# A hybrid decoder layer on one core: another order at its start, a shorter chain for 1/sqrt, and the last column sums on TensorE

## The chip, the core and the metric

The kernel runs on one core of a Trainium2 chip, in one launch. Its engines are TensorE (PE, matrix products), VectorE (DVE), ScalarE (ACT), GpSimd (POOL) and SyncE (SP), which here only issues DMA transfers. Each engine works through its own queue in order; they wait for one another by semaphores. The metric is device time in microseconds (us). Before the change it is 1806.27, the median of three runs.

## The reference

One layer over 1056 positions (1024 of a prompt, 32 of samples), 1024 channels wide, float32 throughout:

```
x = x + 1/2 * SwiGLU_1(RMSNorm(x))          # D_FF = 2816
h = RMSNorm(x);  [q | k | v | u | g] = h @ w_in
    gate = gelu(u) * (tril(W_s) RMSNorm(gelu(g)) + b)      # chunks of 128
    attn = sliding-window attention, 8 heads, ALiBi, sinks
x = x + concat(RMSNorm(attn), RMSNorm(gate)) @ w_out
x = x + 1/2 * SwiGLU_2(RMSNorm(x))
y = RMSNorm(x)                              # the final norm
```

RMSNorm divides each position by the root of the mean square of its channels and multiplies by a gain. SwiGLU is `(silu(h @ wg) * (h @ wu)) @ wd`. The new keys, values and gate rows are outputs too.

## The kernel before

Channels lie on the 128 partitions, in 8 tiles (k); positions lie along the free dimension, in two halves (h = 0, 1) of H = 528, each of two pieces of PC = 264. The three stages are FFN1 (`ffn`, L329, called at L1002), the mixer (projection, attention, gate, output projection) and FFN2 (L1098).

**Products.** A float32 product is done as three products of shorter numbers: each operand is split into a high part (a cast or a scaled copy on ScalarE) and a low part (a subtraction on VectorE). For weights that is `wsplit` (L121 and L122, tiles `raw` to `wb`) and `wload` (`whi`, `wlo`); for the normalised activations it is `P1.split` (L193 writes `xh`, L194 writes `xl`, from x and the gains). A block scheme with seven products in the place of eight (`Blocks`, products `a`, `s1` to `s4`, `12`, `22`) covers the large products. Each product instruction of 128x264 reads one such weight and one such activation.

**1/sqrt.** For a norm, ScalarE squares x (`squares`, L172), the first tile straight into the accumulator, the others into `sq`, which VectorE or GpSimd adds (L176). `rstd` (L143) then lets TensorE sum over the partitions (`pn`, L150), VectorE scales (`gv`, L154 and L155) and calls `tiny_rsqrt` (L133), and TensorE spreads the result over all partitions by products with the identity (`pr`, L165). `tiny_rsqrt` is a guess by integer operations (L136, L137) and three Newton steps of three operations each (L139 to L141), on tiles `gt` and `gr` of 128x5 or smaller. It is called 21 times: 13 from `rstd`, 8 in the gate (tile `gss`, squares `junk` at L814, result used for `gn` at L819).

**The start** (L640 to L662) loads the gains and the first tiles of x and issues ten products of `ones` with itself (`warm`, L645; the profile counts each as two records). It casts the first two weight blocks, splits x for k = 0 to 3, and goes on with the next loads, blocks and splits.

**The end.** FFN2's last group of products runs once for each piece of positions (`pd`, L620); each of its four d steps adds into x on VectorE (L572). `last` and `one` (L1063 to L1096) then square and sum the finished rows and, at d = 3, start `rstd` for the final norm. `put` copies `pr` to `fr` (L1084), VectorE (L1091) and GpSimd (L1089) multiply, and SP stores `y` (L1093). Of three such pieces the last one (piece 2, 264 positions) has no other work beside it.

**What sets the order.** The program text gives priorities only. A scheduler with a cost model places each engine's instructions, inside the mixer together with a table of due times (`I`). So an edit in one place can move instructions of an engine elsewhere.

Of the kernel before, what the change touches and what calls it, by code (L numbers as in the profile page):

```python
# [14 lines left out]
I32 = mybir.dt.int32  # L15
AF = mybir.ActivationFunctionType
ALU = mybir.AluOpType
# [3 lines left out]
D = 1024  # L21
# [19 lines left out]
def build(nc, tc, ctx, A):  # L41
# [16 lines left out]
    V, S, G, PE = nc.vector, nc.scalar, nc.gpsimd, nc.tensor  # L58
# [9 lines left out]
    def tmp(nm, dt=F32):  # L68
        return tp.tile([128, H], dt, tag="tmp", name=nm)

    def pst(nm):
        return ps.tile([128, 512], F32, tag="ps", name=nm)
# [9 lines left out]
    def small(nm, n=4, p=128):  # L82
        return sp.tile([p, n], F32, tag=f"s_{nm}", name=nm, bufs=1 if nm[0] == "s" else 2 if nm[0] == "g" else 3)
# [11 lines left out]
    ones = cp.tile([128, 128], F32, name="ones")  # L95
# [37 lines left out]
    def tiny_rsqrt(a, n):  # L133

        b, c = small("gr", 5)[:, :n], small("gt", 5)[:, :n]
        V.tensor_scalar(c.bitcast(I32), a.bitcast(I32), 1, None, op0=ALU.arith_shift_right)  # L136
        V.tensor_scalar(b.bitcast(I32), c.bitcast(I32), -1, 0x5F3759DF, op0=ALU.mult, op1=ALU.add)  # L137
        for i in range(3):
            V.tensor_mul(c, b, b)  # L139
            V.scalar_tensor_tensor(c, c, -0.5, a, op0=ALU.mult, op1=ALU.mult)  # L140
            V.scalar_tensor_tensor(a if i == 2 else b, c, 1.5, b, op0=ALU.add, op1=ALU.mult)  # L141

    def rstd(acc, o, n, mul, eps, put):  # L143

        full, rest = n // 128, n % 128
        nj = full + (rest > 0)
        p = pst("pn")
        for j in range(nj):
            m = min(128, n - j * 128)
            PE.matmul(p[:m, j:j + 1], lhsT=acc[:, o + j * 128:o + j * 128 + m], rhs=ones[:, 0:1], start=True, stop=True)  # L150
        v = small("gv", 5)
        if rest:
            V.memset(v, 1.0)
            V.tensor_scalar(v[:rest, full:nj], p[:rest, full:nj], mul, eps, op0=ALU.mult, op1=ALU.add)  # L154
        V.tensor_scalar(v[:, :full], p[:, :full], mul, eps, op0=ALU.mult, op1=ALU.add)  # L155
        tiny_rsqrt(v[:, :nj], nj)
        yield 0.3, LAT["rstd"]

        p = pst("pr")
        for j in range(nj):  # L160
            m = min(128, n - j * 128)
            if j == 4:
                put(p, o)
                p = pst("pr2")
            PE.matmul(p[:, j % 4 * 128:j % 4 * 128 + m], lhsT=v[:m, j:j + 1].to_broadcast([m, 128]), rhs=ident[:m, :m], start=True, stop=True)  # L165
        put(p[:, :n] if nj <= 4 else p[:, :rest], o if nj <= 4 else o + 512)
        yield 1.0, 1

    def squares(acc, x, o, n, first, add=None, on=None):
        s = acc[:, o:o + n] if first else tmp("sq")[:, :n]  # L170
        if on is None:
            S.activation(s, x, AF.Square)  # L172
        else:
            on.tensor_mul(s, x, x)
        if not first:
            (add or G).tensor_add(acc[:, o:o + n], acc[:, o:o + n], s)  # L176
# [456 lines left out]
    X = [Quad(f"x{h}", 8) for h in range(2)]  # L633
    P1 = Prep(X, 0, {(1, 3): [0], (2, 2): [1], (2, 3): [0], (2, 7): [1]})
# [5 lines left out]
    load(gains, A["gains"])  # L640
    load_x(0, 0)
    gb_ = Blocks(A["f1_gu"][0, 0], (1, 2))
    pw = pst("warm")
    for _ in range(10):
        PE.matmul(pw[:, :128], lhsT=ones, rhs=ones, start=True, stop=True)  # L645
    load_x(0, 1, 2, 3)
    gb_.load(0, 3)
    gb_.plain("11", "21")
    for k in range(4):
        P1.split(0, k)  # L650
    load_x(0, 4, 5, 6, 7)
    first = [gb_.plain("12", "22")]
# [380 lines left out]
    for job, ahead in zip(jobs, jobs[1:] + [None]):  # L1033
        if job != jobs[0]:
            wnext = weight(*ahead) if ahead else None
        t, h, kind, i = job
# [20 lines left out]
    first = plain_weights(A["f2_gu"])  # L1057
# [3 lines left out]
    fin, ends, pieces = {}, [], [(0, 0, 2), (1, 0, 1), (1, 1, 1)]  # L1061
# [11 lines left out]
    def one(piece, h, o, n, d):  # L1073
        first = piece not in fin
        if first:
            fin[piece] = tmp("facc")
        squares(fin[piece], X[h](d, o, n), 0, n, first, V if piece else G)
        if d != 3:
            return

        def put(p, o2):
            m = p.shape[-1]
            r = tmp("fr")
            S.copy(r[:, :m], p)  # L1084
            for k in range(8):
                x, g = X[h](k, o + o2, m), gains[:, 32 + k:33 + k]
                if k in ON_POOL[piece]:
                    S.activation(x, x, AF.Copy, scale=g)
                    G.tensor_mul(x, x, r[:, :m])  # L1089
                else:  # L1090
                    V.scalar_tensor_tensor(x, x, g, p if piece == 2 else r[:, :m], op0=ALU.mult, op1=ALU.mult)  # L1091
                if k % 2:
                    load(pair(A["y"], k // 2, T0[h] + o + o2, m), X[h].t[k // 2][:, :, o + o2:o + o2 + m])  # L1093
        if piece == 2:
            ends.pop()
        ends.append(rstd(fin[piece], 0, n, 1.0 / D, 1e-6, put))  # L1096

    ffn(X, P2, A["f2_gu"], A["f2_d"], lambda i, h: pair(spill, i, T0[h], H), first, last, tail)  # L1098
    for _ in ends[0]:
# [100 lines left out]
```

## Time and profile before

| | |
|---|---|
| median of 3 runs | 1806.27 us (1805.62, 1806.27, 1806.62) |
| profiled execution | 1804.15 us, of which its span 1802.4 |
| mean granted TensorE clock | 0.99 |
| TensorE busy | 98% of the span |
| VectorE, ScalarE, GpSimd busy | 68%, 41%, 8% |
| HBM traffic | 147 GB/s over the span |

A row of the timeline gives start, busy time, engine, line, operation, `out<-in`, shapes, count, and in brackets the engine's idle time before it with the instruction that ended it. A row of windows gives a stretch, its length, each engine's busy time with its instructions in the order TensorE, its weight loads, VectorE, ScalarE, GpSimd, and then the granted clock, the DMA share and GB/s.

### The profile page before, as it was taken

The numbers are of one execution on the slowest core, as the hardware profiler recorded it, in microseconds if no ns is written. First come the engines' busy times: TensorE is split into PE (matmuls) and PEld (weight loads), VectorE is DVE, ScalarE is ACT, GpSimd is POOL, SyncE is SP. The second block draws the span as 40 slices with busy tenths as digits, with TensorE's granted clock in tenths as the row PEclk, the third lists the DMA queues.
The fourth block names the chain that finished last, engine by engine and source line by source line (L and its number), as shares of the span: only waits on it lengthen the run. The fifth ranks groups of instructions, "written<-read, shape, count | busy, mean of one in ns | idle before, by whom it ended". The sixth has DMA issues, their size and how long they took to land. (4 is left out here: it accounts for less than half of the span.)

```text
span 1802.4 us, 34123 instructions
## 1 busy us (share of the span) xinstructions
PE 1765.7 (98%) x14045; PEld 1729.8 (96%) x14045; DVE 1217.4 (68%) x2171; ACT 740.3 (41%) x1312; POOL 168.6 (9%) x152
## 2 busy tenths in 40 slices
PE   9999999999999999999989999999999999999997
PEld 9999999999999999998878899999999999999997
DVE  7986766676557565486677885986666676457566
ACT  6543333333343453354554644633333333343441
POOL 0000000000000012212212562000000000000110
PEclk9999999999999999999989999999999999999998
DMA  6154544454595344322120222154544454595532
GB/s 237 33 193 160 205 148 149 156 201 140 186 345 179 131 155 144 96 71 64 55 65 28 93 83 95 41 193 157 201 148 154 154 201 137 187 343 188 181 108 97
DMA packets 104460, 266.05 MB, mean 148 GB/s; under 512 B 12384, under 2 KB 15136, under 8 KB 104288
## 3 DMA queue, kind: packets, MB, share of 16 engines
q1 hardware_dynamic: 104304, 263.87, 42.6%
q8 instruction: 110, 1.80, 0.4%
q14 instruction: 46, 0.38, 0.1%
HBM read 190.25 MB, written 74.60 MB: 147 GB/s over the span
## 5 line engine op out<-in xcount | busy, mean ns | idle before, releaser
L430 PE MATMUL pa<-th,wb 128*128 128x264 f32 x2624 | 493.7, 284 | 1.2 <-DVE wb L122 0.6
L430 PEld LDWEIGHTS pa<-th,wb 128*128 128x128 f32 x2624 | 412.3, 188 | 2.6 <-DVE wb L122 0.9
L430 PE MATMUL pa<-tl,wb 128*128 128x264 f32 x1312 | 373.6, 285 | 2.5 <-DVE tl L299 2.5
L620 PE MATMUL pd<-hh,whi 128*128 128x264 f32 x1208 | 343.6, 285 | 0.0
L620 PE MATMUL pd<-hh,wlo 128*128 128x264 f32 x1208 | 343.6, 284 | 0.0
L620 PE MATMUL pd<-hl,whi 128*128 128x264 f32 x1208 | 343.2, 284 | 0.0
L121 ACT CAST wb<-raw 128x512 fp32r<-128x512 f32 x296 | 181.3, 620 | 284.3 <-PE pc L430 82.1
L122 DVE TENSOR_TENSOR wb<-raw,wb 128x512 fp32r<-128x512 f32 x296 | 201.6, 690 | 105.4 <-ACT wb L121 104.8
L430 PEld LDWEIGHTS pa<-tl,wb 128*128 128x128 f32 x1312 | 246.6, 188 | 2.8 <-DVE tl L299 2.7
L430 PE MATMUL pc<-th,wb 128*128 128x264 f32 x1280 | 247.0, 285 | 1.4 <-DVE x L468 0.8
L620 PEld LDWEIGHTS pd<-hh,wlo 128*128 128x128 f32 x1208 | 227.4, 188 | 0.0
L620 PEld LDWEIGHTS pd<-hh,whi 128*128 128x128 f32 x1208 | 227.2, 188 | 0.1
L620 PEld LDWEIGHTS pd<-hl,whi 128*128 128x128 f32 x1208 | 227.2, 188 | 0.0
L430 PEld LDWEIGHTS pc<-th,wb 128*128 128x128 f32 x1280 | 203.3, 188 | 2.0 <-DVE x L468 1.0
L367 DVE TENSOR_TENSOR wlo<-raw,whi 128x1024 fp32r<-128x1024 f32 x82 | 94.7, 1155 | 135.3 <-ACT whi L366 122.5
L430 PE MATMUL pc<-tl,wb 128*128 128x264 f32 x640 | 181.9, 284 | 0.0
L269 DVE TENSOR_TENSOR raw<-raw 128x512 f32<-128x512 f32 x248 | 168.9, 688 | 17.3 <-DMA raw<-f_d 12.3
L366 ACT CAST whi<-raw 128x1024 fp32r<-128x1024 f32 x82 | 79.9, 980 | 217.1 <-PE pd L620 147.0
L130 PE MATMUL pp<-xh,whi 128*128 128x264 f32 x448 | 132.9, 297 | 0.4 <-DVE mx L866 0.4
L130 PE MATMUL pp<-xh,wlo 128*128 128x264 f32 x448 | 128.5, 287 | 0.0
L130 PE MATMUL pp<-xl,whi 128*128 128x264 f32 x448 | 128.2, 286 | 0.0
L430 PEld LDWEIGHTS pc<-tl,wb 128*128 128x128 f32 x640 | 120.3, 188 | 0.3 <-DVE tl L299 0.3
(233 smaller groups left out, 3080.6 us busy)
## 6 DMA issues: line engine op xcount, KB each, us to landing
raw<-f_gu SPq DMA_DIRECT2D x86, 512.0 KB, 4.2
raw<-f_d SPq DMA_DIRECT2D x74, 512.0 KB, 4.0
ws_s<-raw SPq DMA_DIRECT2D x88, 256.0 KB, 2.0
ht<-ht_s SPq DMA_DIRECT2D x40, 528.0 KB, 7.8
raw<-ws_s SPq DMA_DIRECT2D x40, 512.0 KB, 9.0
raw<-w_in SPq DMA_DIRECT2D x28, 512.0 KB, 3.6
ht_s<-m SPq DMA_DIRECT2D x44, 264.0 KB, 2.3
ht<-ht SPq DMA_DIRECT2D x20, 528.0 KB, 3.7
```

The costliest lines, as they stand in the source:

```text
L121: S.copy(w[:, 0], src)
L122: V.tensor_sub(w[:, 1], src, w[:, 0].bitcast(F32))
L130: PE.matmul(p[:, :n], lhsT=w[a][:, c:c + 128], rhs=b(k, o, n), start=(3 * i + j == 0), stop=(3 * i + j == last))
L269: V.tensor_add(b[dst], b[dst], b[x])
L366: S.copy(wh[:, :n * 512], raw[:, :n * 512])
L367: V.tensor_sub(wl[:, :n * 512], raw[:, :n * 512], wh[:, :n * 512].bitcast(F32))
L430: PE.matmul(ps_[:, j], lhsT=w[:, a, kk * 128:(kk + 1) * 128], rhs=b[kk // 2][c][:, kk % 2, j * PC:(j + 1) * PC], start=(start and kk == 0 ...
L620: PE.matmul(ps_[d][:, j], lhsT=w[:, k * 512 + d * 128:k * 512 + (d + 1) * 128], rhs=t[:, k, j * PC:(j + 1) * PC], start=(bi == 0 and oi == ...
```

## The change

1. **Start.** Twelve warm products in the place of ten, by a helper `busy`. The split of x's tile k = 0 is written ahead of the other loads of x and of the weights' casts.
2. **1/sqrt.** Another integer constant and two steps with other constants: nine VectorE operations in the place of eleven, in all 21 calls.
3. **Last piece.** The squares of its last step (d = 3) go to a tile of their own and aren't added by VectorE. TensorE sums the accumulator and then that tile into the same `pn`.
4. **Last piece.** `busy(4)` follows the first group of these sums in the text, `busy(7)` the second.

```diff
-        V.tensor_scalar(b.bitcast(I32), c.bitcast(I32), -1, 0x5F3759DF, op0=ALU.mult, op1=ALU.add)
-        for i in range(3):
-            V.tensor_mul(c, b, b)
-            V.scalar_tensor_tensor(c, c, -0.5, a, op0=ALU.mult, op1=ALU.mult)
-            V.scalar_tensor_tensor(a if i == 2 else b, c, 1.5, b, op0=ALU.add, op1=ALU.mult)
-
-    def rstd(acc, o, n, mul, eps, put):
+        V.tensor_scalar(b.bitcast(I32), c.bitcast(I32), -1, 0x5F1FFFF9, op0=ALU.mult, op1=ALU.add)
+        V.tensor_mul(c, b, b)
+        V.scalar_tensor_tensor(c, c, -0.375 * 0.703952253, a, op0=ALU.mult, op1=ALU.mult)
+        V.scalar_tensor_tensor(b, c, 0.375 * 0.703952253 * 2.38924456, b, op0=ALU.add, op1=ALU.mult)
+        V.tensor_mul(c, b, b)
+        V.scalar_tensor_tensor(c, c, 1 / 0.375 ** 2, a, op0=ALU.mult, op1=ALU.mult)
+        V.scalar_tensor_tensor(c, c, -10.0 / 3.0, c, op0=ALU.add, op1=ALU.mult)
+        V.scalar_tensor_tensor(a, c, 5.0, b, op0=ALU.add, op1=ALU.mult)
+
+    def busy(n):
+        pw = pst("warm")
+        for _ in range(n):
+            PE.matmul(pw[:, :128], lhsT=ones, rhs=ones, start=True, stop=True)
+
+    def rstd(acc, o, n, mul, eps, put, last=None):
...
-        for j in range(nj):
-            m = min(128, n - j * 128)
-            PE.matmul(p[:m, j:j + 1], lhsT=acc[:, o + j * 128:o + j * 128 + m], rhs=ones[:, 0:1], start=True, stop=True)
+        terms = [acc] if last is None else [acc, last]
+        for t, a in enumerate(terms):
+            for j in range(nj):
+                m = min(128, n - j * 128)
+                PE.matmul(p[:m, j:j + 1], lhsT=a[:, o + j * 128:o + j * 128 + m], rhs=ones[:, 0:1], start=(t == 0 and (j == 0 or last is None)),
+                          stop=(t == len(terms) - 1), skip_group_check=last is not None)
+            if last is not None:
+                busy(7 if t else 4)
...
-    pw = pst("warm")
-    for _ in range(10):
-        PE.matmul(pw[:, :128], lhsT=ones, rhs=ones, start=True, stop=True)
+    busy(12)
+    P1.split(0, 0)
     load_x(0, 1, 2, 3)
     gb_.load(0, 3)
     gb_.plain("11", "21")
-    for k in range(4):
+    for k in range(1, 4):
         P1.split(0, k)
...
-        squares(fin[piece], X[h](d, o, n), 0, n, first, V if piece else G)
+        end = None
+        if piece == 2 and d == 3:
+            end = tmp("sq")
+            S.activation(end[:, :n], X[h](d, o, n), AF.Square)
+        else:
+            squares(fin[piece], X[h](d, o, n), 0, n, first, V if piece else G)
...
-        ends.append(rstd(fin[piece], 0, n, 1.0 / D, 1e-6, put))
+        ends.append(rstd(fin[piece], 0, n, 1.0 / D, 1e-6, put, end))
```

Rows of the built programs show what the scheduler makes of it at three places. First ScalarE at the start of the program, before and then with the change (`x_87` and `x_88` are the first tiles of x, `raw` the loaded weights, `acc` and `sq` take squares):

```order
L172 ACTIVATE acc<-x_87 128x528
L121 CAST wb<-raw 128x512 x2
L193 ACTIVATE xh_123<-x_87,gains 128x528 x2
L193 ACTIVATE xh_124<-x_88,gains 128x528 x2
L172 ACTIVATE sq<-x_87 128x528
L121 CAST wb<-raw 128x512 x2
```
```order
L206 ACTIVATE xh_114<-x_87,gains 128x528
L121 CAST wb<-raw 128x512 x2
L206 ACTIVATE xh_114<-x_87,gains 128x528
L185 ACTIVATE acc<-x_87 128x528
L121 CAST wb<-raw 128x512 x2
L206 ACTIVATE xh_115<-x_88,gains 128x528 x2
```

The first `xh` now stands ahead of the casts, and two more casts ahead of the third and fourth `xh`. On SP's queue, before and with the change:

```order
L638 DMA x_87<-x 128x528
L258 DMA raw<-f_gu 128x512 x2
L638 DMA x_87<-x 128x528
L638 DMA x_88<-x 128x528 x2
L258 DMA raw<-f_gu 128x512 x2
L105 DMA raw<-f_gu 128x1024
L638 DMA x_89<-x 128x528 x2
```
```order
L651 DMA x_87<-x 128x528
L271 DMA raw<-f_gu 128x512 x2
L651 DMA x_87<-x 128x528
L271 DMA raw<-f_gu 128x512 x2
L651 DMA x_88<-x 128x528 x2
L105 DMA raw<-f_gu 128x1024 x2
L651 DMA x_89<-x 128x528 x2
```

Two weight blocks moved ahead of the third and fourth tile of x, and one load of 128x1024 more ahead of the fifth. Second, ScalarE in the mixer (exponentials `P,den`, squares `junk` for the gate's 1/sqrt), before and with the change:

```order
L869 ACTIVATE P,den<-P,nm 128x256
L737 ACTIVATE gs<-pv 128x264
L814 ACTIVATE junk,gss<-pt 128x128
L869 ACTIVATE P,den<-P,nm 128x256
L814 ACTIVATE junk,gss<-pt 128x128
L869 ACTIVATE P,den<-P,nm 128x256
L814 ACTIVATE junk,gss<-pt 128x128
L739 ACTIVATE gs<-gs 128x264
L814 ACTIVATE junk,gss<-pt 128x128
L869 ACTIVATE P,den<-P,nm 128x256
L814 ACTIVATE junk,gss<-pt_10716 16x128
L871 ACTIVATE mx<-mx 128x4
```
```order
L749 ACTIVATE gs<-pv 128x264
L826 ACTIVATE junk,gss<-pt 128x128 x4
L826 ACTIVATE junk,gss<-pt_10694 16x128
L751 ACTIVATE gs<-gs 128x264
L881 ACTIVATE P,den<-P,nm 128x256 x4
L883 ACTIVATE mx<-mx 128x4
```

The five squares now stand ahead of the four exponentials. Third, TensorE at the end of the program, before and with the change:

```order
L620 MATMUL pd<-hh,wlg 128x264
L150 MATMUL pn<-ones,facc 128x1 x2
L150 MATMUL pn<-ones,facc 8x1
L165 MATMUL pr<-ident,gv 128x128 x2
L165 MATMUL pr<-ident,gv 128x8
```
```order
L633 MATMUL pd<-hh,wlg 128x264
L160 MATMUL pn<-ones,facc 128x1 x2
L160 MATMUL pn<-ones,facc 8x1
L149 MATMUL warm<-ones 128x128 x5
L160 MATMUL pn<-ones,sq 128x1 x2
L160 MATMUL pn<-ones,sq 8x1
L149 MATMUL warm<-ones 128x128 x6
L178 MATMUL pr<-ident,gv 128x128 x2
L178 MATMUL pr<-ident,gv 128x8
```

Five of the warm products stand between the two groups of sums, six ahead of `pr`.

## The prediction

> **What bounds the kernel now.** I read the busy times on the page first, then the timeline of each engine where TensorE stands, then the granted clock there by windows.
>
> ```profile
> PE 1765.7 (98%) x14045; PEld 1729.8 (96%) x14045; DVE 1217.4 (68%) x2171; ACT 740.3 (41%) x1312; POOL 168.6 (9%) x152
> ```
>
> TensorE is busy for 1765.7 of 1802.4 us, so all other engines together hold it up for 36.7 us (matmul ends are modelled, so this is a rough figure). The change takes no product away. It can only gain where TensorE stands, or where it runs at half clock. I therefore listed TensorE's stops in order of time and kept those with an edited line beside them: the start, the mixer, the tail. First the start, by the timeline of TensorE, ScalarE and VectorE and by windows.
>
> ```profile
> 1.12 4.21 PE L645 MATMUL warm<-ones 128*128 128x128 f32 x20 [1.12 <-DVE gss L812]
> 8.28 1.25 PE L396 MATMUL pg<-xh,wb 128*128 128x264 f32 x4 [2.94 <-ACT xh L193]
> ...
> 9.98 0.42 PE L396 MATMUL pg<-xh,wb 128*128 128x264 f32 x1
> 10.20 0.42 PE L396 MATMUL pg<-xl,wb 128*128 128x264 f32 x1
> ```
> ```profile
> 4.18 0.64 ACT L172 ACTIVATE acc<-x 128x528 f32<-128x528 f32 x1 [2.10 <-DMA x<-x]
> 5.61 0.62 ACT L121 CAST wb<-raw 128x512 fp32r<-128x512 f32 x1 [0.78 <-DMA raw<-f_gu]
> 6.97 0.62 ACT L121 CAST wb<-raw 128x512 fp32r<-128x512 f32 x1 [0.75 <-DMA raw<-f_gu]
> 7.49 2.61 ACT L193 ACTIVATE xh<-x,gains 128x528 fp32r<-128x528 f32 x4
> ```
> ```profile
> 7.62 0.69 DVE L122 TENSOR_TENSOR wb<-raw,wb 128x512 fp32r<-128x512 f32 x1 [0.67 <-ACT wb L121]
> 8.26 2.81 DVE L194 SCALAR_TENSOR_TENSOR xl<-x,gains,xh 128x528 fp32r<-128x528 f32 x4
> ```
> ```profile
> 4.84:8.25 3.41, 0.49 (x5) 0.30 (x3) 1.32 (x2) 1.90 (x4) 0.00 (x0) 0.99 0.94 284
> 8.00:8.50 0.50, 0.23 (x1) 0.23 (x2) 0.50 (x2) 0.50 (x2) 0.00 (x0) 0.65 1.07 407
> 8.50:11.50 3.00, 3.00 (x14) 3.00 (x15) 3.00 (x5) 3.00 (x6) 0.00 (x0) 0.50 1.04 387
> ```
>
> The first product waits 2.94 us for `xh`, which ScalarE writes at 7.49 only because two casts that wait for weights (5.61, 6.97) stand before it, though x had landed by 4.18. Then TensorE runs at clock 0.50 (products 0.22 us apart, the rows of 9.98 and 10.20) until about 11.5; at full clock they are 0.12 apart (1788.61 and 1788.73, quoted at the tail). The drop follows a stretch in which it was busy for 0.49 of 3.41 us. From 8.5 on VectorE and ScalarE are full (3.00 of 3.00) and the DMA share is 1.04, so whatever is put earlier there puts something else later.
>
> **The start, costed.** ScalarE now writes `xh` of the first k-tile of x, then both casts, then the next `xh`; VectorE follows with the low parts. I walk it with the durations above. `xh` (2.61/4) 4.18 to 4.83, its low part (2.81/4) 0.7 behind. The twelve warm matmuls at 0.21 us a record (4.21/20) take 24 records, from 1.12 to 6.2. The first weights are cast 5.61 to 6.23, so the first product goes at about 6.3 instead of 8.28. The second block is cast 6.97 to 7.59, the second `xh` is there by 8.45 and its low part by 9.1: 24 products are done by 10.1. On SP's queue the two next weight blocks (512 KB) now go ahead of x2 and x3, and 512 KB more of up weights ahead of x4 to x7; at 386 to 407 GB/s each is 1.3 us of transfer. By an estimate from these rates x2's and x3's `xh` come at 10.75 and 11.5, with low parts 0.7 behind, and 48 products are done by 14.1. The up weights' products and those of x4 and x5 follow, with short waits for the casts; from about 16.65 TensorE no longer stands, with 70 products done. Before, 1 + 14 were done by 11.5 (the windows' counts) and then one each 0.122 us: 15 + 42 = 57 by 16.65. The difference is 13 products at 0.122: **1.6 us**. If the clock still drops at 8.25, the 9 or so products that no wait for x2 hides pay some 0.07 us more on the mean: 1.0. If x2 to x7 land a further 1 us late: 0.6. If they land 0.6 sooner: 2.2. What comes next (the splits of the other half, up to 28 us) waits for TensorE's and VectorE's order, not for a load, so the shift stays.
>
> **The shorter 1/sqrt** drops two of eleven small VectorE operations at 21 places. Where TensorE does not wait for them it is worth nothing, since its products cover them; that is so in both FFNs apart from their ends. In the mixer it waits at two such places.
>
> ```profile
> 951.05 1.37 PE L165 MATMUL pr<-ident,gv 128*128 128x128 f32 x10
> 955.90 0.39 PE L130 MATMUL pw<-ah,whi 128*128 128x264 f32 x1 [3.48 <-DVE gn L819]
> ...
> 1064.86 1.48 PE L165 MATMUL pr<-ident,gv 128*128 128x128 f32 x10 [1.36 <-DVE gv L141]
> ```
> ```profile
> 951.60 0.17 DVE L816 TENSOR_SCALAR gss<-gss 128x5 f32<-128x5 f32 x1 [0.27 <-ACT junk L814]
> ...
> 954.37 0.17 DVE L141 SCALAR_TENSOR_TENSOR gss<-gt,gr 128x5 f32<-128x5 f32 x1
> ...
> 954.73 1.12 DVE L819 TENSOR_SCALAR gn<-pt,gss 128x128 f32<-128x128 f32 x4
> ...
> 1060.83 1.30 DVE L141 SCALAR_TENSOR_TENSOR gr<-gt,gr 128x5 f32<-128x5 f32 x1
> ...
> 1062.40 0.44 DVE L139 TENSOR_TENSOR gt<-gr 128x5 f32<-128x5 f32 x1
> ...
> 1064.14 0.66 DVE L141 SCALAR_TENSOR_TENSOR gv<-gt,gr 128x5 f32<-128x5 f32 x1
> ```
> ```profile
> 947.61 0.51 ACT L869 ACTIVATE P<-P,nm 128x256 f32<-128x256 f32 x1 [4.57 <-DVE nm L867]
> ...
> 951.22 0.25 ACT L814 ACTIVATE junk<-pt 16x128 f32<-16x128 f32 x1
> ```
> ```profile
> 957.00:960.50 3.50, 3.50 (x17) 3.24 (x16) 2.82 (x9) 0.00 (x0) 1.44 (x2) 0.51 0.00 0
> ```
>
> At 1060 to 1065 these operations take 0.44 to 1.30 us each; two fewer are worth more than the whole wait of 1.36. The end of the wait is then the arrival of other work, so I take 1.2 (0.4, two at 0.2 apart, to 1.36). At 951 the change also moves ScalarE's work: the five squares `junk` come ahead of four exponentials (0.51 each), which in the row of 947.61 stand between them. The last `junk`, now at 951.22, could come 2 us sooner, and `gn` with it; two small operations less add 0.2 to 0.4. But VectorE has other work there and four exponentials come later. Bounds 0 and 2.2; I take 1.2, a little over the middle. The half clock behind it, 957.0 to 960.5, costs 1.7 and I leave it in place. What is behind the late exponentials on VectorE is the scaling of `P` and TensorE's transposes of it, which come after the products of 955.90. Mixer: **2.4** (0.4 to 3.6, with the clock 5.3).
>
> **The tail.** All of it is on the path.
>
> ```profile
> 1788.61 0.28 PE L620 MATMUL pd<-hl,whg 128*128 128x264 f32 x1
> 1788.73 0.28 PE L620 MATMUL pd<-hh,wlg 128*128 128x264 f32 x1
> 1790.56 0.70 PE L150 MATMUL pn<-ones,facc 128*128 128x1 f32 x6 [1.54 <-DVE facc L176]
> 1793.83 1.72 PE L165 MATMUL pr<-ident,gv 128*128 128x128 f32 x6 [2.57 <-DVE gv L141]
> ...
> 1779.83 0.92 PE L165 MATMUL pr<-ident,gv 128*128 128x128 f32 x6
> ```
> ```profile
> 1789.52 0.42 ACT L172 ACTIVATE sq<-x 128x264 f32<-128x264 f32 x1 [3.61 <-DVE x L572]
> ```
> ```profile
> 1789.98 0.43 DVE L176 TENSOR_TENSOR facc<-facc,sq 128x264 f32<-128x264 f32 x1 [0.49 <-ACT sq L172]
> ...
> 1793.33 0.16 DVE L140 SCALAR_TENSOR_TENSOR gt<-gt,gv 128x3 f32<-128x3 f32 x1
> 1793.52 0.16 DVE L141 SCALAR_TENSOR_TENSOR gv<-gt,gr 128x3 f32<-128x3 f32 x1
> ```
> ```profile
> 1789.99:1793.40 3.41, 0.70 (x6) 0.62 (x6) 2.18 (x13) 0.00 (x0) 0.00 (x0) 0.99 0.00 0
> 1793.50:1796.00 2.50, 1.72 (x6) 1.43 (x6) 0.17 (x2) 0.38 (x1) 0.00 (x0) 0.50 0.00 0
> ```
>
> The add of 1789.98 goes, so the last column sums could start at 1790.0 (the square ends at 1789.94) instead of 1790.56: 0.57 saved. But five warm matmuls now stand ahead of them. The first sums run behind the last product (1788.85 to 1789.55), then ten records at 0.11 to 0.14 (1.37/10 in the row of 951.05) until 1790.65 to 1790.95. This gives 0.57 back: net 0.1 to 0.4 lost, at worst; I take 0.1 lost. Two small operations at 0.2 (1793.33 to 1793.52): 0.4 saved. The six warm matmuls behind take until about 1792.7 and do not reach `pr`, due at 1793.5. Then `pr`, 1.72 at clock 0.50, should run at 0.92, as the same six records do at 1779.83: 0.8 saved if the clock holds. Before, it dropped after a stretch with 0.70 busy of 3.41; now that stretch holds 0.7 + 2.5. Tail: -0.1 + 0.4 + 0.8 = **1.1** (0.0 with 0.4 lost and without the clock; 1.8 if the warm matmuls cost nothing: 0.57 + 0.4 + 0.8). The new wait, of the second sums for the square, has only warm matmuls and `pr` queued behind it on TensorE.
>
> The Trainium skill ("TensorE: Matmul & The Clock Gate", Part 1: The HAM clock gate) says that the clock drops after an idle window of about 3.4 us, and that the window runs freely, not counted from the kernel's start. The trace agrees in the length (8.25 to 11.6, 957.0 to 960.5), not in that the window must be idle: 0.49 and 0.70 of 3.41 busy dropped it. By the free-running rule the drop would miss `pr` in some runs before, and the tail's gain would be 0.3 in those.
>
> **The sum.** 1.6 + 2.4 + 1.1 = 5.1 us. The profiled execution took 1804.15 (span 1802.4 and 1.75 around it), 2.1 below the median of 1806.27; the runs lie within 1.0. I subtract from the median: **1801.2**, and 1799.0 for an execution like the profiled one.
>
> **Rivals.** *The mixer gives nothing.* Its order was made by a scheduler and both waits are partly set by other work: POOL shares the 1060s, and at 951 VectorE's other operations fill 4.46 of 4.85 us.
>
> ```profile
> 951.05:955.90 4.85, 1.37 (x12) 1.16 (x11) 4.46 (x30) 3.20 (x16) 0.00 (x0) 1.00 0.00 0
> 1060.00:1063.00 3.00, 3.00 (x27) 3.00 (x26) 2.97 (x6) 1.05 (x1) 2.92 (x4) 1.00 0.31 116
> ```
>
> Then 2.7 is left: 1803.6. Chance 0.18. *The warm matmuls do not do what they say*: the clock drops at both ends all the same, start 1.0, tail 0.3, mixer 0.8 (a third): 1804.2. For it: in the stretch 926.3 to 940.0, quoted below, the clock stayed at 0.50 with TensorE busy for 82% of it. Against: at the start TensorE is now at work nearly all the time from 4.84 to 8.25. Chance 0.12. *Both of the first wait and its half clock go*: mixer 5.3, 8.0 in all: 1798.3. The clock fell after 3.48 idle; with 1.5 it may not. Chance 0.17. *Slower*: a new half-clock stretch in the mixer. One stands in it already:
>
> ```profile
> 926.30:940.00 13.70, 11.19 (x50) 10.52 (x51) 6.69 (x28) 5.08 (x18) 2.38 (x2) 0.50 0.12 40
> ```
>
> It lasted four windows with TensorE 82% busy, and costs 6.85. Moved exponentials that leave TensorE idle in the window from 957 could draw the half clock there out from one window to four: +5.1, and the gain at 951 goes: 1806.27 - 3.9 + 5.1 = 1807.5; with the 0.6 start 1808.5. It decides if a window around 957 to 964 has TensorE about as little busy as the two that dropped the clock above (14% and 20% of 3.41 us). Against it: TensorE is busy for all 3.50 us of the stretch from 957.0, and its products there wait for nothing of the exponentials'. Chance 0.10.
>
> **Numbers.** Main forecast 0.43. What this kernel's measurement tells from no change is 0.2%, 3.6 us, so the border is 1802.7. Faster: 0.9 of 0.43, all of 0.17, and 0.04 of the first rival, whose 1803.6 lies near the border: 0.60. Slower: the last rival comes out within 0.2% by its own price; beyond it, at 1809.9, only with a window more, and I give that and what I don't see 0.07. Same: the rest, 0.33. Range 1797.0 (all upper bounds, 2.2 + 5.3 + 1.8 = 9.3) to 1805.5 (the lower ones, 0.6 + 0.4 + 0.0, and a little); the last rival lies outside.
>
> **What would show it.** Start: first `pg` at 6.3, no clock of 0.50 at 8.5 to 11.5, a wait for x2's `xh` near 10.1. Mixer: `pw` at 951 waits under 2.5, `pr` at 1064 under 0.5. Tail: from the start of the last product to that of the sums over `sq` 1.9 (1.83 before), from there to the end of `gv` 2.7 (3.1 before), `pr` 0.92 long. The prediction is wrong if TensorE's later stages do not keep the start's shift, if a half-clock stretch comes or goes in the mixer, or if the last sums wait for something other than the warm matmuls.

## The result, and the profile after

The changed kernel takes 1795.7 us (median of 6 runs, 1793.65 to 1797.9), the kernel before 1806.08 in the same session (6 runs, 1803.53 to 1808.41): a ratio of 0.9943, 95% interval 0.9931 to 0.9956. A later session gave 0.9935 (0.9921 to 0.9949). The prediction was 1801.2, with a range of 1797.0 to 1805.5. The sign was right; the gain, 10.4 us, is twice the 5.1 forecast and just outside the range. Single executions at a clock of 0.55 to 0.75 took 2130 us and more, among them the one of the changed kernel's second profile; they are left out of all figures here.

The profiled execution took 1793.65 (span 1791.9). The start, by the timelines of ScalarE and of TensorE:

```profile
4.10 1.28 ACT L206 ACT_TABLE_LOAD   x1 [4.10 <-DMA x<-x]
5.39 0.74 ACT L206 ACTIVATE xh<-x,gains 128x528 fp32r<-128x528 f32 x1
6.03 0.60 ACT L121 CAST wb<-raw 128x512 fp32r<-128x512 f32 x1
7.80 0.62 ACT L121 CAST wb<-raw 128x512 fp32r<-128x512 f32 x1 [1.16 <-DMA raw<-f_gu]
```
```profile
1.12 5.47 PE L149 MATMUL warm<-ones 128*128 128x128 f32 x24 [1.12 <-DVE gss L824]
6.69 0.51 PE L409 MATMUL pg<-xh,wb 128*128 128x264 f32 x2
...
8.47 0.39 PE L409 MATMUL pg<-xh,wb 128*128 128x264 f32 x1 [0.97 <-ACT wb L121]
```

The first product goes at 6.69 instead of 8.28. But ScalarE's load of its activation table, 1.28 long, now waits for x until 4.10. Before, it was done long before x landed:

```profile
0.80 1.28 ACT L172 ACT_TABLE_LOAD   x1 [0.80 <-PEq L1182]
```

So the first `xh` comes at 5.39 and not at 4.18. And the second weight block is cast at 7.80 and not at 6.97, so that TensorE waits 0.97 for it.

The mixer, by TensorE's waits from 700 to 1110 us, before and then with the change (columns: who waits for whom, us in total, times, longest):

```profile
PE pn L150 <- POOL oacc L176: 4.1, 1, 4.1
PE po L886 <- ACT PT L882: 3.7, 2, 2.8
PE pw L130 <- DVE gn L819: 3.5, 1, 3.5
PE pg L396 <- DVE wo L981: 2.4, 1, 2.4
PE pr L165 <- DVE gv L141: 1.9, 2, 1.4
```
```profile
PE pn L160 <- POOL oacc L189: 4.2, 1, 4.2
PE po L898 <- ACT PT L894: 3.5, 2, 2.6
PE pg L409 <- DVE wo L993: 2.4, 1, 2.4
...
PE pr L178 <- DVE gv L144: 0.2, 1, 0.2
```

The wait of `pw` for `gn` is gone, and of `pr`'s 1.9 there is 0.2 left; the other large ones stand as they stood. Where the first went, the changed kernel's ScalarE and VectorE timelines show:

```profile
944.51 0.27 ACT L826 ACTIVATE junk<-pt 16x128 f32<-16x128 f32 x1
...
948.52 0.51 ACT L881 ACTIVATE P<-P,nm 128x256 f32<-128x256 f32 x1 [0.65 <-DVE nm L879]
```
```profile
947.75 0.15 DVE L828 TENSOR_SCALAR gss<-gss 128x5 f32<-128x5 f32 x1
...
951.43 0.16 DVE L144 SCALAR_TENSOR_TENSOR gss<-gt,gr 128x5 f32<-128x5 f32 x1
951.77 1.12 DVE L831 TENSOR_SCALAR gn<-pt,gss 128x128 f32<-128x128 f32 x4
```

The last square `junk` runs 4.0 us ahead of the first exponential; before, the first exponential stood at 947.61 and the last square at 951.22, 3.6 behind it. The squares now run in the time in which ScalarE stood idle for `nm` (the 4.57 us in the bracket of the row at 947.61). `gn` starts at 951.77 and not 954.73. So of the 6.7 us by which the last square is earlier, 3.0 reach `gn`: VectorE takes up the squares' sums (`gss`, L828) only at 947.75, behind other work.

That nothing is left of the wait is partly chance. In this execution a half-clock window (3.41 us at a granted clock of 0.50) stands just ahead, so TensorE comes to the place later (`pr` at 952.49, before at 951.05). In the profile of the kernel with the early table load (below), whose ScalarE order here is the same, no such window stands ahead, and 0.62 is left. The window of the changed kernel, and then that stop:

```profile
948.50:951.90 3.40, 3.40 (x18) 3.40 (x17) 3.34 (x25) 3.38 (x14) 0.00 (x0) 0.50 0.01 2
```
```profile
949.89 0.39 PE L130 MATMUL pw<-ah,whi 128*128 128x264 f32 x1 [0.62 <-DVE gn L832]
```

In the kernel before, the wait is 3.48 without a half-clock window ahead and 2.37 with one (its second profile, below). Like against like, the change takes 2.4 to 2.9 off it.

The tail, by TensorE's and VectorE's timelines:

```profile
1779.56 0.63 PE L160 MATMUL pn<-ones,facc 128*128 128x1 f32 x6
1780.12 1.38 PE L149 MATMUL warm<-ones 128*128 128x128 f32 x10
1781.33 0.63 PE L160 MATMUL pn<-ones,sq 128*128 128x1 f32 x6
1781.89 1.61 PE L149 MATMUL warm<-ones 128*128 128x128 f32 x12
...
1784.14 0.99 PE L178 MATMUL pr<-ident,gv 128*128 128x128 f32 x6 [0.64 <-DVE gv L144]
```
```profile
1783.83 0.16 DVE L144 SCALAR_TENSOR_TENSOR gv<-gt,gr 128x3 f32<-128x3 f32 x1
```

The last product starts at 1779.44 (1788.73 before). From there to the end of the span it is 12.5 us, 13.7 before; `pr` takes 0.99 and not 1.72.

**Where the time went.** For each profile I added up TensorE's idle time ahead of its products and the time at half clock up to the last `pr`, by stage. The span is then the idle time, half of the time at half clock and a remainder (1758 to 1759 in both profiles of the kernel before; 1764 with the change, which puts in thirteen more warm products).

| us | before | changed |
|---|---|---|
| idle: start, FFNs, mixer, tail | 4.1, 5.1, 16.6, 4.1 | 2.6, 5.1, 11.0, 0.6 |
| half clock: start, FFNs, mixer, tail | 3.4, 0, 23.9, 2.2 | 0, 3.4, 13.7, 0 |

The mixer lost 5.6 us of idle time and 10.2 us of half clock, worth up to 5.1 (less where TensorE stood anyway). That is up to 10.7 between these two profiles, where the prediction had 2.4; by the places of the same products at 800 and 1105 us it is 9.4. The start's shift of the products is 0.6 at 24 us. A half-clock window near 112 us, new in this execution, cost 1.5. The rest are shifts of under 1 us each.

### The profile page after: what moved, and what is told of

Its sections match the earlier page's. It is cut to its first block, busy times and chain, and to the rows that moved or that the text cites. A ratio compares the mean times of both kernels' runs of the same rounds, so it can differ in the third digit from the quotient of the medians.

```text
span 1791.9 us, 34147 instructions
## 1 busy us (share of the span) xinstructions
PE 1765.9 (99%) x14077; PEld 1730.5 (97%) x14077; DVE 1212.9 (68%) x2128; ACT 741.3 (41%) x1312; POOL 170.0 (9%) x152
## 4 chain that ended last, share of the span: by engine, by line
PE 86%; DVE 6%; issue 5%; ACT 1%; POOL 1%; DMA 0%; SPq 0%; POOLq 0%; DVEq 0%; ACTq 0%
PE pa L443 25%; PE pd L633 22%; PE pc L443 13%; PE pp L130 8%; PE pb L443 6%; PE pg L409 4%; PE pw L130 3%; PE po L898 1%; PE sc L874 1%; DVE tl L312 1%; PE pr L178 1%; DVE wb L122 1%; DVE x L305 1%; PE ptr L893 0%; PE pm L847 0%
## 5 line engine op out<-in xcount | busy, mean ns | idle before, releaser
L282 DVE TENSOR_TENSOR raw<-raw 128x512 f32<-128x512 f32 x248 | 169.5, 691 | 16.4 <-DMA raw<-f_d 11.4
```

The source lines that it names most:

```text
L282: V.tensor_add(b[dst], b[dst], b[x])
```

## The experiments

All in rounds beside the kernel before, whose median lay between 1806.1 and 1808.5 over the sessions; so ratios are compared. Each kernel was profiled once, the one before and the one with the early table load twice: eighteen profiles.

| kernel | median, range (us) | ratio, 95% interval |
|---|---|---|
| changed, again | 1795.7, 1794.5 to 1798.7 | 0.9935, 0.9921 to 0.9949 |
| start alone | 1806.1, 1802.4 to 1809.0 | 0.9987, 0.9973 to 1.0000 |
| short 1/sqrt alone | 1796.6, 1795.6 to 1798.4 | 0.9935, 0.9919 to 0.9951 |
| tail alone | 1807.5, 1801.1 to 1810.8 | 0.9993, 0.9979 to 1.0007 |
| start and tail, long 1/sqrt | 1804.4, 1801.5 to 1806.0 | 0.9983, 0.9971 to 0.9995 |
| one call short (933 us) | 1805.9, 1799.2 to 1808.2 | 0.9987, 0.9974 to 1.0000 |
| one call short (1053 us) | 1805.6, 1802.2 to 1807.8 | 0.9987, 0.9978 to 0.9996 |
| all but 933 and 943 short | 1799.3, 1798.2 to 1800.1 | 0.9957, 0.9944 to 0.9969 |
| all but 1053 short | 1800.4, 1795.0 to 1803.5 | 0.9961, 0.9946 to 0.9975 |
| before, warm at 951 and 1065 | 1805.1, 1802.9 to 1807.8 | 0.9989, 0.9980 to 0.9998 |
| changed, early table load | 1792.3, 1791.9 to 1794.1 | 0.9912, 0.9896 to 0.9928 |
| the same, again | 1794.1, 1791.9 to 1795.9 | 0.9923, 0.9910 to 0.9937 |
| early table, no tail part | 1795.3, 1794.2 to 1796.7 | 0.9935, 0.9922 to 0.9948 |
| early table, warm at 928 | 1788.9, 1788.2 to 1789.5 | 0.9900, 0.9885 to 0.9915 |
| the same, warm at three stops | 1788.8, 1787.5 to 1790.3 | 0.9898, 0.9884 to 0.9912 |
| early table, warm at 928, no busy(4) | 1788.4, 1788.1 to 1790.0 | 0.9894, 0.9881 to 0.9908 |

**The parts alone.** Start alone: the `tiny_rsqrt` and the end of before.

```diff
-    for _ in range(10):
-        PE.matmul(pw[:, :128], lhsT=ones, rhs=ones, start=True, stop=True)
+    busy(12)
+    P1.split(0, 0)
...
-    for k in range(4):
+    for k in range(1, 4):
```

> The kernel before with the first part of the change alone (twelve warm products, the first split ahead of the casts). By the position of the products in the two profiles the start is worth 0.6 us after 24 us, not the 1.6 of the prediction. Theory 'each part is worth what stands beside it': 1805.5, with the half-clock windows of the mixer near 926, 957, 1022 and 1100 all there as before. Rival 'any shift against the free-running clock windows is enough to lose some of them': 1801 to 1803, with two of those windows gone.

Its products are 0.84 us ahead at 24 us, and the median's ratio is worth 2.3 (0.0 to 4.9). The windows near 926, 956, 1021 and 1100 are all there in its profile. The theory stands, within a wide interval.

The short 1/sqrt alone, with the old start and end (the diff of `tiny_rsqrt` as above):

> The kernel before with the shorter 1/sqrt alone. Theory 'the short chain shortens the waits at 951 and 1064 (3.2 and 1.7 us) and with them loses half-clock windows': 1798 to 1799, with the window near 1022 and 1100 gone or half of them. Rival 'the windows are chance': 4.9 for the two waits alone, 1801.2, with as many half-clock windows as before. Prediction's own value for this part: 2.4, so 1803.7.

A ratio of 0.9935: 11.7 us under before (8.9 to 14.6). That is as much as the whole change gives. Its mixer has 11.1 of idle time and 13.7 of half clock, as the whole change has. Both figures of the expectation were too small. The windows near 1022 and 1100 are gone, as the theory has it; but in two other profiles with every call short (the early table load again, and without the tail part) windows stand near 1016 and 1093, so chance has its part in that.

The tail alone, with the long 1/sqrt:

> The kernel before with the last sums on TensorE and the warm products of the tail alone, with the long 1/sqrt. Theory 'clock held in the tail': from the last product to the end 0.8 us shorter than before (13.67), because pr runs in 0.9 and not 1.72, and 0.2 lost or won at the sums: 1805.3. Rival 'the drop of the clock at the end is chance': no difference in the median, 1806.1.

In its profile `pr` takes 0.99, and from the last product to the end of the span it is 12.9 (13.67 before): 0.8, as the theory has it. The median can't tell it from nothing (0.9979 to 1.0007).

Both together, with the long 1/sqrt:

> The changed kernel with the old 1/sqrt of eleven operations: start and tail of the change alone, together. Theory 'the parts add': start 2.0 and tail 1.3 under before by their own medians, so 3.3 under, 1803 to 1804, with the wide spread of the long chain (1799 to 1809). Rival 'the parts gain more together than apart': 10.4 minus 11.5 leaves nothing for start and tail beside the short chain, so 0 to 1.5 under.

3.1 us under before (0.9 to 5.2): the parts add where the chain is long. Beside the short chain, which alone gives 0.9935, no gain of theirs shows in the medians (0.9943 and 0.9935 with them). The intervals are some 5 us wide, so this doesn't show that it is lost there.

**The table load.** One small copy on ScalarE ahead of everything:

```diff
+    S.activation(small("stab", 1), ones[:, 0:1], AF.Copy)
     load(gains, A["gains"])
     load_x(0, 0)
```

> The changed kernel with one small ScalarE copy ahead of everything, so that the load of the activation table, which in the changed kernel waits for x until 4.10 and ends at 5.39, is done before x lands. Theory 'the table load behind x is what the start lost': first xh at 4.2, 1.0 us more gain by 24 us than the changed kernel (1.6 against 0.6): 1794.7. Rival 'the second weight block, landed at 7.8 instead of 6.97, sets the start': first xh earlier but the products after 8.4 at the same times, 0 to 0.3 gained.

ScalarE's timeline of this kernel:

```profile
0.80 1.28 ACT L653 ACT_TABLE_LOAD   x1 [0.80 <-PEq L1200]
2.10 0.20 ACT L653 ACTIVATE stab<-ones 128x1 f32<-128x1 f32 x1
4.01 0.73 ACT L206 ACTIVATE xh<-x,gains 128x528 fp32r<-128x528 f32 x1 [1.72 <-DMA x<-x]
```

The first `xh` comes 1.4 sooner, and at 24 us the products are 1.54 ahead of before, where the changed kernel is 0.6. Not all of that is the table load. The second weight block is cast at 7.35 here and at 7.80 in the changed kernel. And in the kernel of start and tail with the long 1/sqrt the first `xh` comes as late (5.45), but that block is cast at 6.96, and the products are 1.45 ahead. So the rival has its part. One profile of each doesn't settle it, so here are all eighteen: the product at 24.08 us in the profile of before stands at 24.7 on the mean of nine profiles with the old start (24.1 to 25.9), at 23.1 with the new one (three, 22.6 to 23.5) and at 22.6 with the early table load as well (six, 22.2 to 22.8). By these means the new start is worth 1.6 and the early load some 0.6 more; the profile of before has the quickest start of its nine.

The median fell by 3.4, more than the shift, so both were run again in one session:

> The changed kernel again, in one session with the next. Theory 'the early table load is worth its 0.9 us at the start': 0.7 to 1.3 us over the kernel with the early table load. Rival 'it is worth the 3.4 that lie between the two medians so far (1795.7 and 1792.3)': 2.5 to 4 over.

> The changed kernel with the early load of ScalarE's table, again, beside the changed kernel: 0.7 to 1.3 us under it by the shift of the products at 24 us, 2.5 to 4 by the medians so far.

The changed kernel's runs lie from 1794.5 to 1798.7 here, median 1795.7, those with the early table load from 1791.9 to 1795.9, median 1794.1. That is 1.6 lower by the medians and 2.2 by the ratios, and the ranges overlap. A gain of the early load by its shift of some 0.6 fits this; what is beyond it isn't shown.

**Which calls of 1/sqrt.** In the next kernels `tiny_rsqrt` counts its calls and takes the short chain only for those in a list:

```diff
+        calls.append(len(calls))
+        if calls[-1] in SHORT:
+            ...                    # nine operations
+        else:
             ...                    # eleven operations
```

With call 10 alone short (the norm at 933 us) the scheduler already gives ScalarE the changed order at 947 us; with all short but this one and call 11 (the gate's at 943) it keeps the old one. So order and chain can be told apart.

> The kernel before with one of its 21 calls of 1/sqrt shortened, the norm at 933 us; the gate's chain at 951 keeps its eleven operations, but the scheduler gives ScalarE the changed kernel's order there (five squares ahead of the four exponentials). Theory 'the moved ScalarE order is what ends the wait at 951': that wait is under 1 us, the half-clock window behind it (957) is gone, the median lies 5 to 6 us under that of before; the wait of 1.4 at 1065 stays. Rival 'the shorter chain ends it': the wait is 3 or more, the median within 1 us of before.

> The kernel before with 19 of its 21 calls of 1/sqrt shortened, all but the two at 933 and 943 us; the gate's chain at 951 has nine operations and ScalarE keeps the order of before there. Theory 'the moved ScalarE order': the wait at 951 falls by 0.4 at most, to about 3.1, and the wait at 1065 is gone; 2 to 3 us under before. Rival 'the shorter chain': the wait at 951 is under 1.5 and the median 8 to 11 us under before, as with all 21 calls.

Waits of TensorE between 940 and 1070 us, of the kernel with one call short and then of that with nineteen:

```profile
PE pw L130 <- DVE gn L841: 2.4, 2, 1.8
PE pr L189 <- DVE gv L154: 1.4, 1, 1.4
```
```profile
PE pw L130 <- DVE gn L841: 2.9, 1, 2.9
```

The moved order takes the wait for `gn` from 3.5 to 2.4 in two stops, the longer of 1.8; the shorter chain alone takes it to 2.9. Both together leave the 0.6 or nothing seen above. Both theories were too simple here. And the medians go the other way round: nineteen short calls with the stop at 951 still there give 0.9957, one short call with a third of it gone 0.9987. So much of the gain lies at other calls. The norm at 1053 us is one, whose result `pr` waits for at 1065:

> The kernel before with one of its 21 calls of 1/sqrt shortened, the norm at 1053 us whose result TensorE waits for at 1064.86 (1.36 us). ScalarE keeps the order of before at 951. The kernels with all calls long at this place vary by 7 to 10 us from run to run with the granted clock (0.984 to 0.993), those with it short by 2 to 3. Theory 'this wait, where small VectorE operations take up to 1.3 us beside GpSimd, is longer in most runs than in the profile and draws the clock down': spread under 4 us, median 4 to 7 us under before. Rival 'it is worth its profiled 1.36 us': spread as before, 1 to 2 us under.

> The kernel before with 20 of 21 calls of 1/sqrt shortened, all but the norm at 1053 us. Theory 'that call makes the spread': runs vary by 7 us or more again and the median is 4 to 6 us over that of all 21 calls, 1801 to 1803. Rival 'it is worth its 1.36 us': 1798 with a spread of 3 us.

Alone it is worth 2.3 (0.7 to 4.0); taken out of the 21 it costs 4.7 by the ratios (0.9961 against 0.9935, with intervals that just overlap), and the runs spread over 8.5 us again and not 2.8. By these figures it is more than its 1.36 us of wait. But nineteen short calls, this one among them, spread over 1.9 with a long stop at 951, and this one alone over 5.7; so it seems to narrow the spread and doesn't make it by itself (six to twelve runs each). What one call is worth may depend on what the others leave; the intervals are too wide to show it.

**The half clock.** The runs of the kernel before spread over 10 us in one session (1802.25 to 1812.38), and their mean granted clock with them: 0.991 to 0.993 in those under 1803.6, 0.984 in those over 1811.6. Runs of the changed kernel and of the short 1/sqrt alone lie at 0.991 to 0.994. The kernel before once more:

> The kernel before once more, for a second profile of it: at which places its half-clock windows stand when they fall otherwise on the grid. Theory 'the windows run freely': again near 926 and 957, the others shifted, some gone or new (near 112, 1065). Rival 'they belong to the program': the same eight places.

It took 1808.98 (span 1807.3), 4.9 more than the execution of the prediction. The same stretches, by windows, in this second execution and then in the first:

```profile
948.10:954.90 6.80, 6.80 (x27) 5.86 (x26) 5.96 (x34) 5.67 (x28) 0.00 (x0) 0.50 0.00 1
...
958.30:965.20 6.90, 6.12 (x26) 5.86 (x27) 5.28 (x16) 0.00 (x0) 1.44 (x2) 0.51 0.00 0
111.80:115.30 3.50, 3.43 (x15) 3.43 (x16) 3.50 (x7) 0.00 (x0) 0.00 (x0) 0.51 0.86 284
```
```profile
948.10:954.90 6.80, 4.32 (x34) 4.10 (x34) 6.27 (x38) 6.15 (x32) 0.00 (x0) 1.00 0.00 1
957.10:960.50 3.40, 3.40 (x16) 3.14 (x15) 2.72 (x9) 0.00 (x0) 1.44 (x2) 0.50 0.00 0
111.80:115.30 3.50, 3.50 (x30) 3.50 (x30) 3.50 (x7) 1.32 (x3) 0.00 (x0) 1.00 0.91 312
```

Same program, same order, nearly the same stops (28.6 us of idle time, and 29.8 in the first); yet two half-clock windows at 948 and one more each at 958 and 112, and one less near 931. Such a window costs half of its 3.41 us. So a program's time hangs on where the windows fall. Is this the larger part of the gain? The kernel before with warm products in its two stops, chain and order unchanged:

```diff
+        if warm[1]:                       # 6, for the norm before 1065 us
+            busy(warm[1])
         p = pst("pr")
         ...
+        for _ in range(warm[2]):          # 13, for the norm at 951 us
+            PE.matmul(p[:, 128:256], lhsT=ones, rhs=ones, start=True, stop=True)
```

> The kernel before with its long 1/sqrt everywhere and every engine's order, plus warm products in two of TensorE's stops: thirteen behind the products with the identity at 951 us (stop of 3.5, or 2.4 when the clock was low ahead of it) and six ahead of those at 1064.9 (stop of 1.4). The waits stay, only the half-clock windows behind them can go. Theory 'what the two profiles of before don't share, the half clock, is the larger part of the gain of the short 1/sqrt': 4 to 7 us under before. Rival 'the waits are what counts': 0 to 2 us under before. The warm products at 951 may hold up ScalarE's copy of the same tile by some 2 us.

```profile
954.37 1.37 PE L179 MATMUL pr<-ident,gv 128*128 128x128 f32 x10
955.67 3.17 PE L181 MATMUL pr<-ones 128*128 128x128 f32 x26
```
```profile
955.60:959.20 3.60, 3.24 (x28) 3.02 (x27) 3.51 (x22) 2.08 (x9) 0.00 (x0) 1.00 0.00 0
959.20:962.80 3.60, 3.58 (x27) 3.43 (x28) 3.60 (x11) 0.00 (x0) 0.69 (x1) 1.00 0.00 0
```

The clock holds at 1.00 behind the filled stop, and the spread falls to 4.9. But the median is only 2.0 lower (0.4 to 3.6). The theory of 4 to 7 falls: half clock behind these two stops is worth about 2, and the rest of the 11.7 doesn't come from there. These warm products can't reach all of the half clock, though. None of the eighteen profiles has a window of it at 1065, and in two of the five with every call long one stands at 945 to 955, ahead of the stop at 951.

**The other stops.** Sixteen warm products ahead of the sums `pn` at 928 us, on top of the early table load:

```diff
+        if pre:                           # 16, for the norm whose sums stand at 928 us
+            busy(pre)
         p = pst("pn")
```

> The changed kernel with the early table load (1792.3) and sixteen warm products ahead of the sums over oacc near 928 us, where TensorE stands for 4.2 us and three or four half-clock windows follow in every profile so far. Theory 'the stop draws the clock down, and work in it keeps it up': no clock of 0.50 from 925 to 940, 4 to 5 us less, 1787.7. Rival 'the small products behind the stop (transposes and products of 32 columns) draw it down by themselves': one window less at most, 1790.6 to 1792.3.

Windows of 18 us around this stop, without (the early table load alone) and with the warm products:

```profile
923.50:941.50 18.00, 15.05 (x74) 13.09 (x75) 11.41 (x42) 9.01 (x34) 2.82 (x2) 0.72 0.18 52
```
```profile
920.00:938.00 18.00, 16.87 (x121) 14.51 (x120) 15.40 (x54) 12.08 (x40) 4.79 (x3) 1.00 0.12 34
```

The clock stays at 1.00. The gain is 2.2 us by the ratios, or 4.2 from the repeated run (3.4 and 5.1 by the medians). All fifteen profiles without these warm products have half-clock windows here, the three with them none. The stop draws the clock down; the small products behind it don't do it by themselves.

Ten more ahead of the products with `PT` near 1010 and nine ahead of FFN2's first:

> The changed kernel with the early table load and warm products at three stops of TensorE in the mixer and behind it: sixteen near 928 us, ten ahead of the products with PT near 1010 (stop of 2.9), nine ahead of FFN2's first products near 1085 (stop of 2.4). With the first alone 1788.9. Theory 'a stop draws the clock down and work in it keeps it': the half-clock windows near 1010 and 1085 are gone, 1.5 to 3 us less, 1786 to 1787.5. Rival 'they come seldom enough': 1788.5 to 1789, or more where the warm products delay the next ones.

The windows there are gone (no half clock in its mixer at all), and the time is the same, 1788.8. So holding the clock at these two places buys nothing that these medians can tell. It isn't without effect in the profiles: from 1000 to 1089 us the products of this one gain 2.0 on those of the kernel with the first alone, which had a half-clock window at each place. But it had lost 1.5 of that at a window near 110 us, which the other doesn't have.

The tail undone, and `busy(4)` left out:

> The changed kernel with the early table load (1792.3) and without the change's third and fourth part: the last squares are added by VectorE again and there are no warm products at the end. Theory of the ledger (the tail is worth 1.1, most of it the clock of the last products with the identity): 1793.4, those six records at clock 0.50 in 1.7. Rival 'the drop of the clock there is chance': 1792.6, only the 0.2 to 0.4 of the shorter sums lost.

> The changed kernel with the early table load, sixteen warm products near 928 us and without the warm products that busy(4) puts between the two groups of last sums (the scheduler then leaves five between them all the same and two ahead of the last products with the identity). Theory 'two warm products are too few to hold the clock': the last products take 1.2 to 1.7 and not 0.99, 1789.2 to 1789.6, against 1788.9 with them. Rival 'it makes no difference': 1788.9.

Without the tail part `pr` takes 1.35 and the stretch from the last product to the end 12.8, 0.3 to 0.4 more than with it; the time is 2.2 to 4.2 higher by the ratios, against the two runs with the tail. In its profile the difference beyond the tail is half-clock windows at 111 and 1016, so it can't be put down to the tail. Without `busy(4)` five warm products still stand between the sums and two are left ahead of `pr`; it takes 0.99 all the same, and the time is that with six (1788.4 and 1788.9). The theory of too few falls. This kernel is the lowest of all, 18.3 us under before (1.06%, 0.92 to 1.19).

## Why the prediction was wrong

What failed is the mixer: it was forecast at 2.4 and gave some 9, both in idle time and in half clock. The other two terms came out at their size.

- **The start** (1.6 forecast, 0.6 between the two profiles, 1.6 between the means of all profiles). The step "`xh` (2.61/4) 4.18 to 4.83" failed: the first `xh` ran from 5.39. The prediction took ScalarE's first operation as free to start when x lands. The activation table's load belongs to that first operation and here waited for x as well. With the early load 70 products have started by 16.65, as in the walk (though without its wait for x2's `xh` near 10.1). That the late load left 1.6 on the means is in part luck: the walk was counted from the quickest of nine old starts. That the clock would no longer drop at 8.25 was right. Eight of the nine profiles with the old start have a half-clock window from 8.1 to 9.4 us on, none of the nine with the new one.
- **The wait at 1065** (1.2 forecast). Right: gone, 1.36 us, and with its surroundings a shift of 1.7 in the positions of the products.
- **The wait at 951** (1.2 forecast, bounds 0 and 2.2). This step failed most plainly: 3.48 became nothing, or 0.62 without a half-clock window ahead, a gain of 2.4 to 2.9. "The last `junk`, now at 951.22, could come 2 us sooner" kept ScalarE's start at 947.61. But the quoted row itself says that ScalarE stood idle 4.57 us before it, for `nm`. A square that no longer stands behind that wait starts in the idle time, 6.7 us earlier (944.51 against 951.22, with TensorE's products near 944 at most 0.4 us earlier). The bound counted the work removed ahead and forgot the wait removed ahead. That VectorE has other work there, as the prediction said, is why only 3.0 of the 6.7 reached `gn`.
- **"The half clock behind it, 957.0 to 960.5, costs 1.7 and I leave it in place"** failed by size. In the mixer the time at half clock went from 23.9 to 13.7 us in the two profiles, worth up to 5.1, where the sum had nothing. The window at 957 went, one came at 948.5, and those at 1022 and 1100 went. So the prediction's own sign of being wrong, a half-clock stretch that comes or goes in the mixer, was there; but the two profiles of the kernel before differ in such stretches too. The rival in which wait and half clock both go was the nearest: its 1798.3 is 2.6 above the result.
- **The tail** (1.1 forecast). The profile gives 1.2, with `pr` at 0.99, sums over `sq` 1.89 behind the last product (1.9 forecast) and 2.66 from there to the end of `gv` (2.7 forecast). Right. In all ten profiles with the old tail `pr` runs at half clock, in one for 0.94 of its 1.35 us and else throughout; in the eight with the new tail it never does.
- **The sum against one execution.** I subtracted what one profile shows from the median, and took the runs' spread of 1.0 (three runs) for the kernel's. In later sessions the kernel before spread over 7 to 10 us, and its second profile has 10.5 us more of half clock than the first. So one profile is a poor price list. It doesn't explain the mixer's 2.4, though: there the profile of the prediction lies near the mean of five.

The means of several profiles share out the gain. Five have every call long (before twice, start alone, tail alone, both together), and five every call short without warm products in the mixer (changed, short 1/sqrt alone, early table load twice, the same without the tail part). From 600 us to 12 us behind FFN2's first products:

| us, mean (lowest to highest) | every call long | every call short |
|---|---|---|
| idle time of TensorE | 16.1 (15.4 to 16.6) | 11.4 (11.0 to 11.9) |
| half clock | 24.6 (17.1 to 30.7) | 16.4 (13.7 to 20.5) |

That is 4.7 of idle time and 8.2 of half clock, worth 4.1: 8.8 in the mixer. With 0.4 in the tail the short chain comes to 9.2, inside the interval of its 11.7 (8.9 to 14.6). With 1.6 for the start and 0.8 for the rest of the tail it is 11.6 in all, where the changed kernel measured 10.3 and 11.7 by its two ratios.

What stays open: why the half clock is less with the short chain beyond the two stops. Warm products in these, with the waits kept, brought about 2. One short call brought 2.3 in each of two cases, each with a wide interval; leaving the one at 1053 long costs 4.7, and leaving those at 933 and 943 long costs 4.0, with intervals that overlap that of all 21 short. How one stop decides what a later one costs wasn't isolated.

## What to carry to other kernels

When an operation is moved ahead of a wait on its engine, its new time is set by what it waits for itself; the bracket of the row that stood ahead of it tells how much idle time it can move into. What hangs on it gains only as much as the next engine's order lets through, here 3.0 of 6.7 us. An operation that becomes the first on ScalarE brings the table load with it, and what it waits for may be waited for by the load: a small first operation that waits for no transfer takes the load out of the way. And where a stop of one engine draws the clock down, price it from several executions, not from one; the start, too, looked worth 0.6 between two profiles and 1.6 between the means.

## What was not expected of the hardware

- The table load waited for the DMA of x and then took 1.28 us ahead of the first `xh` (4.10 to 5.39); with a first operation that waits for no DMA it ran from 0.80. Before the change it ran from 0.80 too, ahead of a square that waits for x alone, where `xh` reads x and the gains. What decides whether the load waits isn't shown.
- The same program on the same kind of chip took 1802.25 to 1812.38 us in one session, with a mean granted clock of 0.993 to 0.984: the half-clock windows, 3.41 us each, fell differently in each execution. The Trainium skill ("TensorE: Matmul & The Clock Gate", Part 1: The HAM clock gate) says that the window runs freely and doesn't start with the kernel; the two profiles of the kernel before agree (windows from 926.3 and 957.1 in one, from 931.0, 948.1 and 958.3 in the other). The same section of the Trainium skill puts the penalty of the ramp from the low clock at under 1% of a typical kernel's span. The spread here, 10 us of 1806, is 0.6%.
- A window at half clock followed stops of 2.4 to 2.5 us (near 109 us) in six of the eighteen profiles, so less than a whole idle window is enough. Thirteen warm products held the clock through a stop of 3.5 us (one profile), sixteen through one of 4.2 (three profiles).
